# RWKV-7 recurrence in chunks of 64 tokens, with the triangular inverse from 16x16 blocks and two block doublings on TensorE

## The chip, the cores and the metric

The kernel runs on one core of a Trainium2 chip. The metric is the device time of one launch in microseconds. The engines are TensorE (PE in the rows, its weight loads PEld), VectorE (DVE), ScalarE (ACT), GpSimd (POOL) and SyncE (SP), which here only issues transfers.

## The reference, cut to what matters

A decoder layer on 1024 tokens: a projection, then a dilated attention branch and an RWKV-7 branch, which are gated, merged and projected. The change touches the RWKV branch alone, and in it the recurrence over the tokens, for 8 heads of 64 channels:

```
def rwkv7_scan(r, decay, k, v, a_in, b_in):
    def step(state, inp):
        r_t, w_t, k_t, v_t, a_t, b_t = inp
        sa = jnp.einsum('bhvk,bhk->bhv', state, a_t)
        state = (state * w_t[:, :, None, :] + sa[..., None] * b_t[:, :, None, :]
                 + v_t[..., None] * k_t[:, :, None, :])
        y = jnp.einsum('bhvk,bhk->bhv', state, r_t)
        return state, y
    _, ys = lax.scan(step, s0, xs)
```

with a_in = -kk and b_in = kk * a. The kernel does this in chunks of C tokens. Inside a chunk the tokens' influence on one another is a triangular system: with the strictly triangular C x C matrix of products of kk and kk * a (weighted with the decays), the contributions u of the chunk are the inverse of (one minus that matrix) times a right hand side made from the state and from v. So for each head and chunk a unit triangular matrix of C x C is inverted, ahead of the chain, since it depends on no state.

## The kernel before, in words

`start` normalises x and transposes it, `bias_table` builds tables, `rwkv` does the RWKV branch, `attention` and `finish` do the rest. In `rwkv` the 1024 tokens are 8 segments of SEG = 128, each of CPS = SEG / C = 4 chunks of C = 32. Heads are held in pairs (NPAIR = 4), one head on partitions 0 to 63, the other on 64 to 127.

For each segment s there are five steps. `rwkv_inputs` makes r, k, v, decays and the normalised kk: matmuls L495, L447, L451 and L456, with work of VectorE, ScalarE and GpSimd between them, in single buffers named kk, aa, c, q, sig and so on (`t_`). `rwkv_gram` makes ar and bk, multiplies them for each chunk and head (L557, 32 matmuls, in two halves), masks the products into gt (L558) and inverts. The inverse before: gt's triangular quarter goes to DRAM (L562, tin_d) and comes back with one matrix of 32 x 32 on each of 32 partitions (L565, xinv); 30 pairs of VectorE instructions, L570 (multiply into xtmp) and L572 (add into xinv), eliminate column by column; the result goes to DRAM (L575, x_d) and comes back as tt, laid out for TensorE (L578). `rwkv_rows` transposes bw and v (L593, L600) into bkt and uv (L597, L603), and has the bonus (L605). `rwkv_chain` goes through the chunks in order: right hand side from uv and the state (L626, L629), copied to rhs_s (L632, L633); u = tt times it (L636), copied to uv (L638, L639); the new state (L642, L645); y (L647, L650). Each of these is 8 matmuls, one for each head, which the trace shows as 16 records (a float32 matmul has two; a transpose has one). `rwkv_post` normalises y and stores it (L662 to L678).

The order is made by a scheduler, from priorities: in round i the chain of segment i has the highest, then come post of i - 1, rows of i + 1, inputs and gram of i + 2. What TensorE does beside it is projection work for later stages, called fill here: matmuls of 128 x 512 (L146), 624 of which are tied to the chain by `issue_after`, spread evenly over the marks that `rwkv_chain` returns (four for each chunk), 78 for each segment. A projection over half of the tokens, in records of 256 columns (L161), and the first fills run ahead of the chain. Each engine takes its instructions in the order that the scheduler wrote. PSUM has three buffers for the matmuls of inputs, gram, rows and post (ps_g), and one for y (ps_y).

Of the kernel before, what the change touches and what calls it, by code (L numbers as in the profile page):

```python
# [17 lines left out]
P = 128  # L18
# [4 lines left out]
NH = 8  # L23
# [11 lines left out]
C = 32  # L35
# [39 lines left out]
def constant_tables():  # L75
# [13 lines left out]
    i = np.arange(P)[:, None] % 64  # L89
    t = np.arange(64)[None, :]  # L90
    src, dst = i % 32, t % 32
    gmask = (np.where(t < 32, src < dst, src <= dst) * np.where(i < 32, -1.0, 1.0)).astype(np.float32)
# [4 lines left out]
    return dict(onehot=onehot.reshape(32, 1152), fill=fill.reshape(1, 1152), gmask=gmask, sel=sel.reshape(8, 512))  # L97


class Kernel:  # L100
# [154 lines left out]
    def small_loads(self):  # L255
# [28 lines left out]
        self.gmask = self.small.tile([P, 64], F32, name="gmask")  # L284
        nc.sync.dma_start(self.gmask, a["gmask"])
# [27 lines left out]
    def rwkv(self):  # L313
# [5 lines left out]
        with ExitStack() as ctx:  # L319
# [8 lines left out]
            nc.vector.memset(self.sgn, 1.0)  # L328
            nc.vector.memset(self.sgn[0:32], -1.0)
            nc.vector.memset(self.sgn[64:96], -1.0)  # L330
# [23 lines left out]
            for i in range(3):  # L354
                self.gt.append(rc.tile([P, NPAIR, CPS, 2, C], F32, name=f"gt{i}"))
            for i in range(2):
                self.tt.append(rc.tile([P, NPAIR, CPS, C], F32, name=f"tt{i}"))
            self.st = self.rw.tile([P, NPAIR, HD], F32, name="state", tag="state", bufs=2)
# [3 lines left out]
            raw = self.rw.tile([P, 1 + S], F32, name="waraw", tag="xinv")  # L362
# [158 lines left out]
    def rwkv_gram(self, sg):  # L521
# [26 lines left out]
        halves = (slice(0, 64), slice(64, 128))  # L548
        nh = NH * CPS
        tin_d = self.dram.tile([nh, C, C], F32, name=f"tin_d{s}")  # L550
        gm = self.gmask.rearrange("p (b t) -> p b t", t=C)[:, None].to_broadcast([P, 2 * CPS, 2, C])
        for p0 in (0, 2):
            ps = self.ps_g.tile([P, 2, CPS, 2 * C], F32, name="pg", tag="pg")
            for p in range(2):
                for ch in range(CPS):
                    for h in halves:
                        nc.tensor.matmul(ps[h, p, ch], bk[h, p0 + p, ch], ar[h, p0 + p, ch], start=True, stop=True)  # L557
            nc.vector.tensor_tensor(gt[:, p0:p0 + 2].rearrange("p a c b t -> p (a c) b t"),  # L558
                                    ps.rearrange("p a c (b t) -> p (a c) b t", t=C), gm, ALU.mult)
        for h in range(2):  # L560
            i0 = h * nh // 2
            nc.sync.dma_start(tin_d[i0:i0 + nh // 2].rearrange("c s t -> s c t"),  # L562
                              gt[h * 64:h * 64 + C, :, :, 0].rearrange("p a c t -> p (a c) t"))
        x = self.rw.tile([nh, C, C], F32, name="xinv", tag="xinv", bufs=1)
        nc.sync.dma_start(x, tin_d)  # L565
        tm = self.rw.tile([nh, 240], F32, name="xtmp", tag="xtmp", bufs=1)
        for j in range(1, C - 1):
            n = C - 1 - j
            o = tm[:, :j * n].rearrange("p (m n) -> p m n", n=n)
            nc.vector.tensor_tensor(o, x[:, 0:j, j:j + 1].to_broadcast([nh, j, n]),  # L570
                                    x[:, j:j + 1, j + 1:].to_broadcast([nh, j, n]), ALU.mult)
            nc.vector.tensor_tensor(x[:, 0:j, j + 1:], x[:, 0:j, j + 1:], o, ALU.add)  # L572
        nc.vector.memset(x.rearrange("p s t -> p (s t)")[:, 0:C * C:C + 1], 1.0)
        x_d = self.dram.tile([nh, C, C], F32, name=f"x_d{s}")
        nc.sync.dma_start(x_d, x)  # L575
        for h in range(2):
            i0 = h * nh // 2
            nc.sync.dma_start(tt[h * 64:h * 64 + C].rearrange("p a c t -> p (a c) t"),  # L578
                              x_d[i0:i0 + nh // 2].rearrange("c s t -> s c t"))
        sg.update(ar=ar, gt=gt, bw=bw, tt=tt)  # L580

    def rwkv_rows(self, sg):
# [4 lines left out]
        bkt = self.rw.tile([P, NPAIR, CPS, HD], F32, name="bkt", tag="bkt", bufs=2)  # L587
        uv = self.rw.tile([P, NPAIR, CPS, HD], F32, name="uv", tag="uv", bufs=2)
        for p0 in (0, 2):
            ps = self.ps_g.tile([P, 2, CPS // 2, 2, HD], F32, name="pg", tag="pg")  # L590
            for p in range(2):
                for j in range(CPS // 2):
                    nc.tensor.transpose(ps[:, p, j].rearrange("p h c -> p (h c)"),  # L593
                                        bw[p0 // 2][:, p, 2 * j:2 * j + 2].rearrange("p c t -> p (c t)"), self.ident)
            for par, rows in enumerate(halves):
                for h, out in enumerate(halves):
                    nc.scalar.activation(bkt[out, p0:p0 + 2, par::2], ps[rows, :, :, h], AF.Copy, scale=self.sgn[rows])  # L597
# [3 lines left out]
        for ch in range(CPS):  # L601
            for h in range(2):
                nc.scalar.copy(uv[64 * h + C:64 * h + 2 * C, :, ch], ps[ch * C:ch * C + C, :, h * HD:h * HD + HD])  # L603
# [464 lines left out]
```

## Time and profile before

| what | us |
|---|---|
| median of 3 runs | 1517.81 (1513.37 to 1521.56) |
| profiled execution | 1511.61 |
| its span | 1509.8 |

The page's mean granted clock of TensorE is 0.959 of full speed. Over the whole span TensorE is busy for 1391.1 us (92%), VectorE for 927.6 (61%), ScalarE for 583.7 (39%), GpSimd for 526.8 (35%). Busy shares over the whole span mix stages; the recurrence is the stretch from about 123 to 618 us, and what is done to it is read there. "Idle before" in a row is the time in which the engine stood still just ahead of it, with the instruction or transfer that ended it. The clock of a window is the mean granted one: 1.00 is 2.4 GHz, 0.50 is 1.2 GHz.

### The profile page before, as it was taken

The numbers are of one execution on the slowest core, as the hardware profiler recorded it, in microseconds if no ns is written. First come the engines' busy times: TensorE is split into PE (matmuls) and PEld (weight loads), VectorE is DVE, ScalarE is ACT, GpSimd is POOL, SyncE is SP. The second block draws the span as 40 slices with busy tenths as digits, with TensorE's granted clock in tenths as the row PEclk, the third lists the DMA queues.
The fourth block names the chain that finished last, engine by engine and source line by source line (L and its number), as shares of the span: only waits on it lengthen the run. The fifth ranks groups of instructions, "written<-read, shape, count | busy, mean of one in ns | idle before, by whom it ended". The sixth has DMA issues, their size and how long they took to land.

```text
span 1509.8 us, 24964 instructions
## 1 busy us (share of the span) xinstructions
PE 1391.1 (92%) x9566; PEld 1148.4 (76%) x9566; DVE 927.6 (61%) x1930; ACT 583.7 (39%) x1361; POOL 526.8 (35%) x418
## 2 busy tenths in 40 slices
PE   4989988999879989999999899989998999898997
PEld 3889876777657667787887788768876888786886
DVE  5213888869787784355548754875477447846723
ACT  4435472555526543134432543354235422002311
POOL 1347644355346343232222322222123123553300
PEclk9999998998879899999999999999999999999999
DMA  7665333121122122221112111221122114674306
GB/s 161 162 189 148 107 99 99 57 72 46 54 64 62 48 54 58 87 56 43 35 45 69 54 49 40 59 69 43 37 63 67 29 43 157 202 236 147 98 26 170
DMA packets 180715, 128.36 MB, mean 85 GB/s; under 512 B 35428, under 2 KB 160828, under 8 KB 180596
## 3 DMA queue, kind: packets, MB, share of 16 engines
q1 hardware_dynamic: 180596, 126.77, 30.4%
q8 instruction: 75, 1.23, 0.4%
q14 instruction: 44, 0.36, 0.1%
HBM read 99.13 MB, written 32.32 MB: 87 GB/s over the span
## 4 chain that ended last, share of the span: by engine, by line
PE 58%; DVE 20%; DMA 10%; ACT 4%; issue 3%; POOL 2%; SPq 1%; DVEq 0%; POOLq 0%; ACTq 0%
PE acc L146 32%; PE acc L161 4%; DMA wb<-wd 3%; DVE xtmp L570 3%; DVE xinv L572 2%; PE acc L1009 2%; PE acc L1010 2%; PE acc L1008 2%; DMA wstage<-in_w_in_dram 2%; DVE q L759 1%; PE rhs L647 1%; PE pw L855 1%; DMA wstage<-in_w_out_dram 1%; PE upd L636 1%; DVE L L782 1%
## 5 line engine op out<-in xcount | busy, mean ns | idle before, releaser
L125 POOL TENSOR_TENSOR wlo<-wstage,whi 128x512 fp32r<-128x512 f32 x186 | 255.0, 1373 | 545.2 <-DVE whi L122 294.7
L146 PE MATMUL acc<-hh,whi 128*128 128x512 f32 x976 | 398.2, 408 | 12.4 <-DVE q L759 7.5
L146 PE MATMUL acc<-hh,wlo 128*128 128x512 f32 x976 | 395.8, 406 | 0.9 <-POOL wlo L125 0.9
L146 PE MATMUL acc<-hl,whi 128*128 128x512 f32 x976 | 394.6, 405 | 0.0
L146 PEld LDWEIGHTS acc<-hh,whi 128*128 128x128 f32 x976 | 188.6, 193 | 52.9 <-issue 6.6
L146 PEld LDWEIGHTS acc<-hh,wlo 128*128 128x128 f32 x976 | 188.4, 193 | 39.4 <-POOL wlo L125 1.8
L146 PEld LDWEIGHTS acc<-hl,whi 128*128 128x128 f32 x976 | 188.5, 193 | 37.6 <-issue 0.3
L570 DVE TENSOR_TENSOR xtmp<-xinv 32x30 f32<-32x30 f32 (+14 forms) x240 | 115.6, 482 | 24.1 <-DMA xinv<-tin_d 18.3
L788 ACT ACTIVATE L<-L,nm 128x128 f32<-128x128 f32 (+1 forms) x192 | 83.8, 438 | 80.4 <-DVE nm L785 80.1
L782 DVE CUSTOM_DVE_ANT_0 L<-pw,bias 128x128 f32<-128x128 f32 (+1 forms) x192 | 62.3, 348 | 83.3 <-PE pw L781 82.8
L572 DVE TENSOR_TENSOR xinv<-xinv,xtmp 32x30 f32<-32x30 f32 (+14 forms) x240 | 109.8, 457 | 6.0
L122 DVE CAST whi<-wstage 128x512 fp32r<-128x512 f32 x108 | 54.5, 505 | 63.1 <-PE acc L146 26.4
L161 PE MATMUL acc<-hh,wlo 128*128 128x256 f32 x384 | 81.3, 294 | 5.4 <-POOL wlo L125 5.4
L767 POOL CAST k<-k 64x512 fp32r<-64x512 f32 x48 | 47.2, 982 | 106.3 <-ACT k L766 105.4
L124 ACT CAST whi<-wstage 128x512 fp32r<-128x512 f32 x78 | 48.2, 619 | 91.0 <-PE acc L161 30.7
L161 PE MATMUL acc<-hl,whi 128*128 128x256 f32 x384 | 83.1, 295 | 0.0
L161 PE MATMUL acc<-hh,whi 128*128 128x256 f32 x384 | 81.1, 293 | 0.2 <-ACT whi L124 0.2
L758 ACT ACTIVATE q<-acc 64x512 fp32r<-64x512 f32 x48 | 41.9, 907 | 94.1 <-PE pw L781 67.0
L858 ACT CAST ph<-pw 128x512 fp32r<-128x512 f32 x72 | 41.5, 578 | 84.5 <-PE pv L867 64.1
L780 PE MATMUL pw<-k,q 128*128 128x128 f32 (+1 forms) x192 | 52.1, 286 | 20.3 <-DVE st L782 20.1
L161 PEld LDWEIGHTS acc<-hh,wlo 128*128 128x128 f32 x384 | 61.9, 197 | 7.1 <-POOL wlo L125 6.0
L859 DVE TENSOR_TENSOR pl<-pw,ph 128x512 fp32r<-128x512 f32 x72 | 47.9, 670 | 30.9 <-ACT ph L858 30.5
(220 smaller groups left out, 2604.8 us busy)
## 6 DMA issues: line engine op xcount, KB each, us to landing
wstage<-in_w_in_dram SPq DMA_DIRECT2D x170, 256.0 KB
x<-in_x_dram SPq DMA_DIRECT2D x32, 256.0 KB
raw<-raw_d SPq DMA_DIRECT2D x24, 258.0 KB
raw_d<-rv SPq DMA_DIRECT2D x24, 256.0 KB
wb<-wd SPq DMA_DIRECT2D x24, 256.0 KB
bias_d<-bias_r SPq DMA_DIRECT2D x24, 192.0 KB
tb_d<-tb SPq DMA_DIRECT2D x16, 256.0 KB
ga_d<-tb SPq DMA_DIRECT2D x16, 256.0 KB
```

Of the source, the lines that this page charges most:

```text
L122: self.nc.vector.tensor_copy(hi, x)
L124: self.nc.scalar.copy(hi, x)
L125: self.nc.gpsimd.tensor_tensor(lo, x, hi.bitcast(F32), ALU.subtract)
L146: nc.tensor.matmul(ps, wt, x[:, k], start=k == 0 and j == 0, stop=k == KT - 1 and j == 2)
L161: nc.tensor.matmul(ps[:, half * 256:half * 256 + 256], wt, part(half, x, k), start=k == 0 and j == 0 and half == 0, stop=k == KT - 1 and j ...
L570: nc.vector.tensor_tensor(o, x[:, 0:j, j:j + 1].to_broadcast([nh, j, n]), x[:, j:j + 1, j + 1:].to_broadcast([nh, j, n]), ALU.mult)
L572: nc.vector.tensor_tensor(x[:, 0:j, j + 1:], x[:, 0:j, j + 1:], o, ALU.add)
L767: nc.gpsimd.tensor_copy(self.gview(ks2[h][b], g, half), hi.bitcast(F32))
L780: nc.tensor.matmul(ps[:, :w], qs2[h][:, qc], ks2[h][:, kc], start=True, stop=False)
L782: nc.vector.tensor_tensor_reduce(l[:, l0:l0 + w], ps[:, :w], self.bias[h][:, bo:bo + w], 1.0, -3.0e38, ALU.add, ALU.max, st[:, gi, 0, h, n ...
L788: nc.scalar.activation(ls, ls, AF.Exp, bias=nm[:, n:n + 1], scale=1.0, accum_out=st[:, gi, 1, h, n:n + 1])
L859: nc.vector.tensor_tensor(pl[:, :cw], ps[:, :cw], ph[:, :cw].bitcast(F32), ALU.subtract)
```

## The change

C becomes 64, so CPS becomes 2. A chunk's matrices are 64 x 64; the masks and the layouts of gt, uv, bkt follow, and the two heads of a pair lie crosswise, so that one matmul of the chain takes 64 rows and 128 columns (L677) and the state's part comes in two halves (L681). The marks for the fill are four for each chunk as before, so eight for each segment instead of sixteen. PSUM: ps_g has two buffers, y has two (rhs0, rhs1).

The inverse is a function of its own. The 64 x 64 matrices (16 in a segment) are cut into their four 16 x 16 diagonal blocks, which go to 64 partitions (four loads, L592) and are eliminated in 14 pairs of VectorE instructions (L597, L599). The blocks go back to DRAM (four stores, L602) into an x_d that is zero elsewhere, and come in as xd in TensorE's layout (L606). Then two doublings: transpose on VectorE (L608), multiply with gt (L612), mask (L613), multiply (L616), add (L617): now there are blocks of 32; transpose (L619), multiply (L623), copy (L626), multiply (L629), copy (L632): blocks of 64. These tiles take buffers that exist already: xd that of kk, xt that of aa, xq that of c, xinv that of ys. The diff's core:

```diff
-C = 32
+C = 64
-            self.ps_g = pool(name="ps_g", bufs=3, space=PSUM)
+            self.ps_g = pool(name="ps_g", bufs=2, space=PSUM)
-                self.gt.append(rc.tile([P, NPAIR, CPS, 2, C], F32, name=f"gt{i}"))
+                self.gt.append(rc.tile([P, 2, NPAIR, CPS, 2 * C], F32, name=f"gt{i}"))
+            self.x_d = [self.dram.tile([NH * CPS, C, C], F32, name=f"x_d{i}") for i in range(2)]
...
-            ps = self.ps_g.tile([P, 2, CPS, 2 * C], F32, name="pg", tag="pg")
-            for p in range(2):
-                for ch in range(CPS):
-                    for h in halves:
-                        nc.tensor.matmul(ps[h, p, ch], bk[h, p0 + p, ch], ar[h, p0 + p, ch], start=True, stop=True)
+            ps = [self.ps_g.tile([P, 2, CPS, 2 * C], F32, name="pg", tag="pg") for _ in range(2)]
+            for p, ch, i, j in itertools.product(range(2), range(CPS), range(2), range(2)):
+                for h in range(2):
+                    u, w = (own[i], own[1 - i])[h], (own[j], own[1 - j])[h]
+                    nc.tensor.matmul(ps[h][u, p, ch, w], bk[own[h], p0 + p, ch, own[1 - i]],
+                                     ar[own[h], p0 + p, ch, own[1 - j]], start=True, stop=True)
...
-        x = self.rw.tile([nh, C, C], F32, name="xinv", tag="xinv", bufs=1)
-        nc.sync.dma_start(x, tin_d)
+        x = self.rw.tile([nb * nm, 16, 16], F32, name="xinv", tag="ys")
+        block = lambda d, j: d[:, 16 * j:16 * j + 16, 16 * j:16 * j + 16]
+        for j in range(nb):
+            nc.sync.dma_start(x[j * nm:(j + 1) * nm], block(tin_d, j))
-        for j in range(1, C - 1):
-            n = C - 1 - j
+        for j in range(1, 15):
+            n = 15 - j
             o = tm[:, :j * n].rearrange("p (m n) -> p m n", n=n)
...
-        nc.sync.dma_start(x_d, x)
+        for j in range(nb):
+            nc.sync.dma_start(block(x_d, j), x[j * nm:(j + 1) * nm])
+        sq = lambda name, tag: self.rw.tile([P, NPAIR, CPS, C], F32, name=name, tag=tag)
+        d, dt, qt = sq("xd", "kk"), sq("xt", "aa"), sq("xq", "c")
         for h in range(2):
-            i0 = h * nh // 2
-            nc.sync.dma_start(tt[h * 64:h * 64 + C].rearrange("p a c t -> p (a c) t"),
-                              x_d[i0:i0 + nh // 2].rearrange("c s t -> s c t"))
+            nc.sync.dma_start(rows(d, h), half(x_d, h))
+        nc.vector.transpose(flat(dt), flat(d))
+        ps = psum()
+        for p, ch, h in each:
+            nc.tensor.matmul(ps[own[h], p, ch], gt[own[h], h, p, ch, own[h]], dt[own[h], p, ch], start=True, stop=True)
+        nc.vector.tensor_tensor(qt, ps, self.lmask[:, None, None].to_broadcast([P, NPAIR, CPS, C]), ALU.mult)
+        ps = psum()
+        for p, ch, h in each:
+            nc.tensor.matmul(ps[own[h], p, ch], qt[own[h], p, ch], d[own[h], p, ch], start=True, stop=True)
+        nc.vector.tensor_tensor(tt, ps, d, ALU.add)
+        dt = sq("xt", "aa")
+        nc.vector.transpose(flat(dt), flat(tt))
+        ps, qt = psum(), sq("xq", "c")
+        for p, ch, h in each:
+            nc.tensor.matmul(ps[hi[h], p, ch, 0:32], gt[lo[h], h, p, ch, hi[h]], dt[lo[h], p, ch, 0:32], start=True,
+                             stop=True)
+        for h in range(2):
+            nc.scalar.copy(qt[hi[h], :, :, 0:32], ps[hi[h], :, :, 0:32])
+        ps = psum()
+        for p, ch, h in each:
+            nc.tensor.matmul(ps[lo[h], p, ch, 32:64], qt[hi[h], p, ch, 0:32], tt[hi[h], p, ch, 32:64], start=True,
+                             stop=True)
+        for h in range(2):
+            nc.scalar.copy(tt[lo[h], :, :, 32:64], ps[lo[h], :, :, 32:64])
...
+            for p, h, w, u in each:
+                nc.tensor.matmul(py[h][:, p], gt[u, h, p, ch, w], uv[w, p, h, ch], start=p == 0, stop=False,
+                                 skip_group_check=True)
```

The change moves instructions on every engine. On TensorE, in the middle of the recurrence (segment 3 to 7 alike), before: the transposes of post and rows (L672, L593) stand between pieces of a chain (L642, L647) and fill (L146).

```order
L146 MATMUL acc<-hh_123,wlo 128x512
L647 MATMUL rhs<-uv,gt_428 32x64
L642 MATMUL snew<-uv,bkt 64x64 x8
L647 MATMUL rhs<-uv,gt_428 32x64 x6
L672 MATMUL pg<-ident,d 128x128 x4
L593 MATMUL pg<-ident,bw 128x128 x8
L647 MATMUL rhs<-uv,gt_428 32x64
L146 MATMUL acc<-hh_123,whi 128x512
```

The same place now: the last fill (L154), the four steps of an inverse (L612 to L629), rows (L644 to L655) and the first two steps of the chain that uses this inverse (its gt is the same, gt_429).

```order
L154 MATMUL acc<-hl_126,whi 128x512
L612 MATMUL pg<-xt,gt_429 64x64 x16
L616 MATMUL pg<-xd,xq 64x64 x16
L623 MATMUL pg<-xt,gt_429 32x32 x16
L629 MATMUL pg<-tt_431,xq 32x32
L725 MATMUL pg<-ident,d 128x128 x4
L629 MATMUL pg<-tt_431,xq 32x32 x15
L644 MATMUL pg<-ident,bw 128x128 x8
L650 MATMUL pg<-ident,v 128x128 x4
L655 MATMUL pg<-r,blk 128x512
L677 MATMUL rhs<-uv,gt_429 128x64 x4
L681 MATMUL rhs<-state,ar 64x64 x7
```

No matmul of the chain or of the fill stands between the steps of the inverse any more. On SP's queue, before: an inverse's two stores and one load go out, other transfers follow (tables L423, post L678, weights L113), then the store and the two loads of its result.

```order
L562 DMA tin_d_4660<-gt_428 32x16x32 x2
L565 DMA xinv<-tin_d_4660 32x1024
L423 DMA tb_d<-tb 128x512
L678 DMA orw_d<-ys 128x4x128
L113 DMA wstage<-in_w_in_dram 128x4x128
L423 DMA tb_d<-tb 128x512
L113 DMA wstage<-in_w_in_dram 128x4x128
L575 DMA x_d_4763<-xinv 32x1024
L578 DMA tt_430<-x_d_4763 32x16x32 x2
```

SP's queue now, at the same place in a segment.

```order
L121 DMA wstage<-in_w_in_dram 128x4x128
L588 DMA tin_d_5397<-gt_427 64x8x64 x2
L437 DMA tb_d<-tb 128x512
L592 DMA xinv<-tin_d_5397 16x16x16 x4
L602 DMA x_d_432<-xinv 16x16x16 x4
L606 DMA xd<-x_d_432 64x8x64 x2
L731 DMA orw_d<-ys 128x4x128
```

The store of x_d follows the load of xinv directly, post's store (L731) comes behind the loads of xd, and an inverse has twelve transfers in place of six.

## Rows read from the trace of the kernel before

**Rows 1.** Windows: length, busy of each engine (instructions), PEclk, DMA share, GB/s.

```profile
206.00:618.00 412.00, 373.86 (x3999) 286.11 (x3997) 305.41 (x701) 195.86 (x475) 182.35 (x155) 0.91 0.23 63
```

**Rows 2.** Timeline of TensorE, the ends of stages: start, length, instruction, records.

```profile
123.43 1.71 PE L495 MATMUL pg<-wa,waup 64*128 64x128 f32 x16
...
149.87 2.08 PE L557 MATMUL pg<-ar,bk 64*64 64x64 f32 x64
...
206.50 0.68 PE L629 MATMUL rhs<-state,ar 64*64 64x64 f32 x16
...
278.40 0.68 PE L626 MATMUL rhs<-uv,gt 32*64 32x64 f32 x16
...
618.03 0.63 PE L647 MATMUL rhs<-uv,gt 32*32 32x64 f32 x14
```

**Rows 3.** Groups, 206 to 618 us, VectorE: busy, mean ns, idle before.

```profile
L570 DVE TENSOR_TENSOR xtmp<-xinv 32x30 f32<-32x30 f32 (+14 forms) x210 | 97.7, 465 | 20.8 <-DMA xinv<-tin_d 16.0
L572 DVE TENSOR_TENSOR xinv<-xinv,xtmp 32x30 f32<-32x30 f32 (+14 forms) x210 | 93.6, 446 | 5.2
```

**Rows 4.** Waits of TensorE, 206 to 575 us: total, times, longest.

```profile
PE upd L636 <- DVE rhs_s L632: 16.5, 8, 4.1
```

**Rows 5.** Chain of work that ended last: start, length, what.

```profile
380.64 2.73 DMA x_d<-xinv
...
383.85 2.15 DMA tt<-x_d
...
435.54 2.57 DMA tin_d<-gt
438.17 2.20 DMA xinv<-tin_d
...
441.12 0.22 DVE xinv L572
441.37 0.24 DVE xtmp L570
```

**Rows 6.** Groups with shapes kept apart, 206 to 618 us.

```profile
L558 DVE TENSOR_TENSOR gt<-pg,gmask 128x512 f32<-128x512 f32 x12 | 8.0, 679 | 0.8 <-PE pg L557 0.8
L503 DVE TENSOR_TENSOR_SCAN c<-smask,sig 128x512 f32<-128x512 f32 x6 | 7.2, 1208 | 0.0
L603 ACT COPY uv<-pg 32x256 f32<-32x256 f32 x56 | 20.4, 364 | 0.7
```

**Rows 7.** Timeline of TensorE, inside segments.

```profile
397.80 2.15 PE L495 MATMUL pg<-wa,waup 64*128 64x128 f32 x16
...
427.56 2.08 PE L557 MATMUL pg<-ar,bk 64*64 64x64 f32 x64
...
499.77 0.93 PE L593 MATMUL pg<-ident,bw 128*128 128x128 f32 x7
...
505.16 1.16 PE L495 MATMUL pg<-wa,waup 64*128 64x128 f32 x8 [0.45 <-ACT bkt L597]
...
616.18 0.39 PE L146 MATMUL acc<-hl,whi 128*128 128x512 f32 x1
616.41 0.40 PE L146 MATMUL acc<-hh,wlo 128*128 128x512 f32 x1
```

**Rows 8.** Timeline of SP's queue.

```profile
495.13 0.86 SPq L562 DMA_DIRECT2D tin_d<-gt  x2
497.93 0.31 SPq L565 DMA_DIRECT2D xinv<-tin_d  x1
```

**Rows 9.** Windows around a wait of TensorE, columns as in rows 1.

```profile
379.00:386.00 7.00, 0.39 (x2) 0.17 (x2) 2.80 (x9) 0.99 (x2) 2.68 (x2) 0.75 0.54 131
386.00:394.00 8.00, 7.87 (x64) 6.47 (x65) 5.52 (x17) 5.03 (x12) 2.79 (x3) 0.58 0.23 68
```

**Rows 10.** Timeline of TensorE at that wait.

```profile
385.47 0.39 PE L636 MATMUL upd<-rhs_s,tt 32*32 32x64 f32 x2 [6.98 <-DMA tt<-x_d]
386.13 1.03 PE L636 MATMUL upd<-rhs_s,tt 32*32 32x64 f32 x14 [0.28 <-DMA tt<-x_d]
```

More of the change, by code (lines that the diff above doesn't have):

```diff
@@ L582, in rwkv_rows @@
+        for h in range(2):
+            nc.scalar.copy(tt[lo[h], :, :, 32:64], ps[lo[h], :, :, 32:64])
     def rwkv_rows(self, sg):
@@ L586, in rwkv_rows @@
         halves = (slice(0, 64), slice(64, 128))
[L587 to L597, printed above, removed]
+        bkt = self.rw.tile([P, NPAIR, 2, CPS, HD], F32, name="bkt", tag="bkt", bufs=2)
+        uv = self.rw.tile([P, NPAIR, 2, CPS, HD], F32, name="uv", tag="uv", bufs=2)
+        for ch in range(CPS):
+            ps = self.ps_g.tile([P, NPAIR, P], F32, name="pg", tag="pg")
+            for p in range(NPAIR):
+                nc.tensor.transpose(ps[:, p], bw[p // 2][:, p % 2, ch], self.ident)
+            nc.scalar.activation(bkt[:, :, 1, ch], ps[:, :, HD:], AF.Copy, scale=self.sgn)
+            nc.scalar.activation(bkt[halves[1], :, 0, ch], ps[halves[0], :, 0:HD], AF.Copy, scale=-1.0)
+            nc.scalar.copy(bkt[halves[0], :, 0, ch], ps[halves[1], :, 0:HD])
         ps = self.ps_g.tile([P, NPAIR, SEG], F32, name="pg", tag="pg")
@@ L602, in rwkv_rows @@
             for h in range(2):
[L603 removed]
+                nc.scalar.copy(uv[halves[h], :, h, ch], ps[halves[ch], :, h * HD:h * HD + HD])
         ps = self.ps_g.tile([P, NPAIR, SEG], F32, name="pg", tag="pg")
@@ L614, in rwkv_chain @@
         sg["yt"] = yt
-        hs = ((slice(0, 64), slice(0, 32), slice(32, 64)), (slice(64, 128), slice(64, 96), slice(96, 128)))
-        each = [(p, *h) for p in range(NPAIR) for h in hs]
+        own = (slice(0, C), slice(C, 2 * C))
+        each = [(p, h, own[h], own[1 - h]) for p in range(NPAIR) for h in range(2)]
         marks = []
@@ L628, in rwkv_chain @@
-            for p, h, u, w in each:
-                last = nc.tensor.matmul(py[h, p], ar[h, p, ch], st[h, p], start=False, stop=False,
-                                        skip_group_check=True)
-            marks.append(last.ins)
-            nc.vector.tensor_copy(rs[0:C], py[0:C])
-            nc.scalar.copy(rs[64:64 + C], py[64:64 + C])
+            for p, h, w, u in each:
+                nc.tensor.matmul(py[h][:, p], gt[w, h, p, ch], uv[w, p, h, ch], start=p == 0, stop=False,
+                                 skip_group_check=True)
@@ L634, in rwkv_chain @@
+            for part in range(2):
+                for p, h, w, u in each:
+                    last = nc.tensor.matmul(py[h][(u, w)[part], p], ar[w, p, ch, own[part]], st[w, p], start=False,
+                                            stop=False, skip_group_check=True)
+                if part == 0:
+                    marks.append(last.ins)
+            nc.vector.tensor_copy(rs[own[0]], py[1][own[0]])
+            nc.scalar.copy(rs[own[1]], py[0][own[1]])
             ps = self.ps_ch.tile([P, NPAIR, HD], F32, name="upd", tag="ch")
-            for p, h, u, w in each:
+            for p, h, w, u in each:
@@ L645, in rwkv_chain @@
             nc.vector.tensor_tensor(sn, ps, sw, ALU.add)
-            for p, h, u, w in each:
-                last = nc.tensor.matmul(py[w, p], gt[u, p, ch, 1], uv[u, p, ch], start=False, stop=True,
+            for p, h, w, u in each:
+                last = nc.tensor.matmul(py[h][w, p], gt[u, h, p, ch, w], uv[u, p, h, ch], start=False, stop=True,
                                         skip_group_check=True)
-            for i, (_, _, w) in enumerate(hs):
-                nc.scalar.copy(yt[ch * C:ch * C + C, :, i], py[w])
+            for h in range(2):
+                nc.scalar.copy(yt[ch * C:ch * C + C, :, h], py[h][own[h]])
             self.st = sn
```

83 lines of the change are left out of this document (49 added, 34 removed).

## The prediction

> **What bounds the kernel now.** I read the windows first, to find the stage, then the timeline of TensorE, to see what paces it, then the groups and waits, to see who is late. The recurrence and its inverses run from the first matmul of `rwkv_inputs` at 123.4 us to the last y matmul (L647) at 618.0 [rows 1, 2]. What follows on TensorE follows at once and is not touched by the change, so a shift of that end moves the total by as much. The chain starts at 206.5 and closes eight segments in 412 us, 51.5 us a segment [rows 1, 2]. In these 412 us TensorE is busy for 374, VectorE for 305, at a mean granted clock of 0.91 [rows 1]. Of VectorE's 305 us the inverse alone (L570 and L572, 7 segments) has 97.7 + 93.6 = 191 us, some 27 us a segment [rows 3]. The chain waits for VectorE in consequence: `upd` waited 16.5 us in all for the rhs_s copy [rows 4]. So neither engine is the bound alone. TensorE's work fills most of it, and the waits of the chain fill the rest. What keeps it at 51.5 is that three segments are in flight: the inverse of s+2 runs beside the chain of s.
>
> **The change part by part.**
>
> *VectorE.* 60 small steps a segment become 28. Two steps follow each other in 0.25 us [rows 5], so 28 take about 6.5 us where about 27 went: some 20 us a segment are taken off VectorE. It gains two more gt evacuations, a multiply, an add (0.68 each, L558's row) and two transposes [rows 6]. No transpose is in the trace. Between a 32x256 copy of 0.36 us and a 128x512 scan of 1.21 us [rows 6] I take 0.9, since its operands are 128x512.
>
> *The chain.* Per 64 tokens 2 x 5 bursts of 16 records become 6 bursts, of which L677 has tiles of 64 by 128. A full burst takes 0.61 us from the start of one to the next (L626 at 278.40, 0.68 us long) [rows 2]; L677 lies between that and the 1.71 us of L495, whose tiles are 64 by 128 with 128 columns for 64 [rows 2]. I take 0.86, near half of L495, and 4.3 us for a chunk of 64 tokens. As to small tiles, 16 records at 32x64 (278.40) and 16 at 64x64 (206.50) both took 0.68 [rows 2], so going from tiles of 32 to tiles of 64 costs nothing by the rows. The Trainium skill, in TensorEngine Tiling (Array Packing), section Key Properties, has different tiles loading weights and multiplying in parallel, and section Overview counts 16 tiles at 32x32 and 4 at 64x64. By that rule alone L677, with two tiles for four, would take 1.2 us instead of my 0.86, some 6 us over 16 chunks, and the trace, where 8 and 4 tiles took the same time, does not bear it out.
>
> *The gram.* Twice the matmuls: 128 records a segment for 64, which took 2.08 [rows 7]: 4.2 us, and the gt evacuation of the later half, 2 x 0.68 = 1.4, before the inverse may load.
>
> *The order.* This is the heart of it. The tiles of the new inverse, xd, xt, xq and xinv, lie in the buffers kk, aa, c and ys, which `rwkv_inputs` and `rwkv_post` write. So the inputs of segment s+1 can't write aa, kk and c before the inverse of s is done with them, and the order after shows what that brings: in each of segments 3 to 7 the inverse of s stands last, right behind the second half of its gram and 17 or 19 fill matmuls; then come rows of s and the chain of s, with the inputs and the gram of s+1 among them. Before, the inverse of s+2 ran while the chain of s had TensorE. Now nothing of TensorE lies beside the round trip through DRAM but 4 us of fill (19 x 0.23, the fill's distance from 616.18 to 616.41 [rows 7]). One period is a loop through five things, and I sum them from the end of one inverse to the end of the next.
>
> H, from the end of the inverse to the first input matmul: before, L593 at 499.77 to L495 at 505.16, 5.4 us, for the same transposes and evacuations [rows 7].
>
> I, from that matmul to the end of the second gram half. At the stage's beginning, with no chain beside it, 123.43 to 149.87, 26.4 us, to the start of the gram [rows 2]; in a busy segment 397.80 to 427.56, 29.8 [rows 7]; plus the gram's 4.2 with half its work on the first half. TensorE's own list in it comes to the same: 61 fill x 0.23 = 14, two chunks of the chain without the fill 8.6, the inputs' matmuls 4, the gram 4.2. I take 32, between 27 and 36.
>
> G, the gt evacuation: 1.4.
>
> R, the round trip. Before: 435.54 (tin_d) to the first step behind the load, 4.8 us (2.57 + 2.20 and their joints); back, 380.64 to 386.0, 5.4 us [rows 5]. An issue on SP takes 0.31 to 0.43 [rows 8]; three more loads of xinv and three more stores of x_d stand in a row, 2 x 3 x 0.43 = 2.6. With 28 steps, 6.5: 19.3. The pieces are 64 bytes now in place of 128 for tin_d and 4 KB for xinv. In the trace the 128-byte pieces landed in 2.57 us and the 4-KB rows in 2.20 [rows 5], 0.4 apart, so I add nothing. The Trainium skill, in DMA: Bandwidth & Descriptors, section Specifications, says that transfers under 512 B are read, modified and written. By that rule the four passes would be dearer, by 0.4 each if the trace's difference is its price, 1.6 us a segment; no row shows more.
>
> T, the first transpose: 0.9.
>
> S, four bursts of 32 records (L612, L616, L623, L629) with a multiply, an add, a transpose and 2 x 2 copies of 0.36 [rows 6] between them, each step waiting for the one ahead. At the full clock a burst takes 1.24 (twice 0.61). But TensorE has then waited some 18 us. Before, it waited 6.98 us for the same transfer to tt, and the granted clock of the next 8 us was 0.58, mostly the lower level of 1.2 GHz; 14 records went in 0.96 us, 0.069 each [rows 9, 10]. So 32 records take 2.2 us: 8.8 + 0.68 + 0.68 + 0.9 + 1.4 + 1.0 for seven joints of 0.15 = 13.5 (9.6 at the full clock).
>
> P = 5.4 + 32 + 1.4 + 19.3 + 0.9 + 13.5 = 72.5 us a segment, for 51.5 now. The 20 us that VectorE is relieved of don't appear: its steps were beside the chain, and what they cost there, 16.5 us of waiting in all, is less than one period's growth.
>
> *The first segments.* Gram 0 starts at 149.9 as now, with 25 fill records of the span's 256 columns (0.115 each, half of 0.23) between its halves, and ends at 157; gt 158.4; R + T to 178.6; TensorE comes to L612 by 157 + 202 x 0.115 = 180; S with 84 such records among it: the inverse of segment 0 ends at 198. Segment 1: inputs to gram 26.4, gram and gt 5.6, R + T + S 33.7: 262 to 264. Segment 2 is the first full period, and has 19 fills before its end: 337. So the inverse of 7 ends at 337 + 5 x 72.5 = 699.5. Behind it 4 us of rows and two chunks of 39 fills (9.0) and 4.3 each: 730 us. Before it was 618. That is +112.
>
> **Sum.** 1511.6 us, the profiled run, + 112 = 1623. The median shown is 0.4% above that run; 6 us are inside the range.
>
> **The rivals.** *Slower, but less: the clock stays at 2.4 GHz.* Then S is 9.6 and I 28: P 64.6, the end near 682, 1576 us. For it: the clock recovered within 8 us before [rows 9]. Against: every period has its own wait of 18 us.
>
> *Slower, and more: each pass in small pieces is dearer*, by 1 us for each of the six added DMAs: P 78.5, 1653 us. For it: nothing in the trace has 64-byte pieces.
>
> *Faster: the round trip is covered.* If the inverse of s lies beside the chain of s-1 as now, the loop is set by TensorE's list: about 32 for I, 5.4 for the rows, 7.5 for the bursts of the inverse and what of G is left: P 45. End: 337 + 225 + 30.6 = 593, 26 us earlier, 1486. It decides at P = (618 - 30.6 - 337) / 5 = 50.1: G + R + T + S would have to fall from 35 to 13. For it: VectorE is relieved of 20 us and `upd` waited 16.5 for it [rows 3, 4]. Against: the shared buffers forbid it, and the order has no chain matmul beside the round trip.
>
> *No change*: P between 48.6 and 51.6 by both at once, part covered and part not. Nothing speaks for just this.
>
> **How the numbers follow.** Forecast (P 66 to 76, some 1590 to 1641) 0.72; the full clock 0.11; dearer pieces 0.10; faster 0.04; no change 0.03. For the range I take the bounds: P = 61 (I 27, R 17 with the issues hidden, S 9.6) gives 1566, P = 84 (I 36, R 24, S 15.5, H 6.5) gives 1681. Half a per cent, 7.6 us, is about what a measurement of this kernel can tell from no change. Faster by more 0.04, within 0.03, slower 0.93.
>
> **What would show it.** In the trace of the changed kernel: segments of the chain 65 to 80 us apart; TensorE idle for 15 to 20 us ahead of each L612, ended by the transposed xd or its DMA; a clock near 0.5 in the bursts behind it; VectorE's L597 and L599 at some 45 us for seven segments, in unbroken rows of 0.25 us; burst L677 near 0.86. Wrong it would be if chain matmuls fill the time ahead of L612, if the load behind tin_d lands in much over 3 us, or if inputs to gram take under 25 us once VectorE is free.

## The result and the profile after

The changed kernel takes 1693.3 us (median of 4 runs, 1684.77 to 1697.18), the kernel before 1519.7 beside it: a ratio of 1.114, interval 1.108 to 1.120. The forecast was 1623, range 1566 to 1681. The direction was right and the loss much larger, +174 us for a forecast +112.

The loss lies in the recurrence alone. Its last y matmul ends at 803 us where [rows 2] had 618, and the stretch behind it is as long as before. Windows of the changed kernel (length, busy of PE, PEld, DVE, ACT, POOL with instructions, clock, DMA share, GB/s), the stage from the old start of the chain to its end, and the rest:

```profile
206.00:803.00 597.00, 440.19 (x4366) 351.12 (x4364) 199.86 (x487) 170.08 (x423) 174.21 (x144) 0.72 0.17 43
803.00:1692.00 889.00, 844.69 (x4205) 702.78 (x4203) 523.39 (x1045) 294.26 (x716) 248.62 (x184) 0.98 0.28 81
```

Against [rows 1] TensorE is busy for 74% of the stage instead of 91%, at a clock of 0.72 instead of 0.91. VectorE is indeed relieved: 200 us in 597, for 305 in 412. What ends TensorE's idle time is one thing. Waits of TensorE from 120 to 800 us (total, times, longest), the first three:

```profile
PE pg L612 <- DVE xt L608: 120.3, 8, 21.7
PE pg L623 <- DVE xt L619: 11.4, 7, 1.6
PE pg L568 <- POOL bk L550: 7.3, 1, 7.3
```

And the timeline of L612, segments 3, 4, 5 and 7 (start, length, instruction, records, idle before):

```profile
430.31 1.97 PE L612 MATMUL pg<-xt,gt 64*64 64x64 f32 x32 [18.02 <-DVE xt L608]
510.17 1.97 PE L612 MATMUL pg<-xt,gt 64*64 64x64 f32 x32 [18.47 <-DVE xt L608]
593.68 1.97 PE L612 MATMUL pg<-xt,gt 64*64 64x64 f32 x32 [20.35 <-DVE xt L608]
...
753.53 1.76 PE L612 MATMUL pg<-xt,gt 64*64 64x64 f32 x28 [15.97 <-DVE xt L608]
```

Four segments from 430.31 to 753.53: 80.8 us each, and 16 to 22 us of each are an idle TensorE, where the forecast expected it. One segment in the prediction's parts, as windows: H, the two pieces of I (split where the clock changes), R with T, and S.

```profile
442.60:450.30 7.70, 7.42 (x32) 4.91 (x32) 0.81 (x2) 3.84 (x10) 2.71 (x3) 0.50 0.11 34
450.30:466.00 15.70, 15.70 (x88) 13.32 (x87) 3.10 (x7) 7.05 (x19) 5.39 (x4) 0.59 0.11 34
466.00:488.30 22.30, 22.30 (x311) 17.89 (x309) 13.64 (x22) 6.29 (x14) 14.36 (x13) 1.00 0.23 63
...
490.00:510.20 20.20, 1.73 (x10) 1.12 (x9) 6.14 (x31) 0.00 (x0) 0.00 (x0) 0.60 0.22 45
510.20:522.40 12.20, 8.48 (x136) 7.02 (x136) 3.48 (x5) 5.36 (x14) 1.19 (x1) 0.50 0.00 1
```

R and S are as forecast. H and I are not: after the idle TensorE the clock stays at its lower level of 1.2 GHz through S, through H and through the first half of I, some 30 us, until well after TensorE is busy without a gap (15.70 us of 15.70, at 0.59). The round trip itself, in the chain of work that ended last (start, length, what):

```profile
490.15 2.62 DMA tin_d<-gt
...
494.20 2.01 DMA xinv<-tin_d
...
497.56 0.21 DVE xtmp L597
497.79 0.21 DVE xinv L599
...
503.96 1.70 DMA x_d<-xinv
...
506.38 2.83 DMA xd<-x_d
...
509.31 0.72 DVE xt L608
```

### The profile page after: what moved, and what is told of

Read it like the earlier page. It is cut to its first block, busy times and chain, and to the rows that moved or that the text cites. A ratio compares the mean times of both kernels' runs of the same rounds, so it can differ in the third digit from the quotient of the medians.

```text
span 1692.7 us, 25693 instructions
## 1 busy us (share of the span) xinstructions
PE 1463.2 (86%) x10078; PEld 1220.8 (72%) x10078; DVE 789.9 (47%) x1674; ACT 549.6 (32%) x1281; POOL 508.3 (30%) x402
## 4 chain that ended last, share of the span: by engine, by line
PE 52%; DVE 16%; DMA 9%; ACT 4%; issue 2%; SPq 2%; POOL 1%; DVEq 0%; ACTq 0%; POOLq 0%
PE acc L154 29%; DMA wb<-wd 2%; PE rhs L677 2%; PE acc L1062 2%; PE acc L1063 2%; PE acc L1061 2%; PE rhs L681 2%; DMA tin_d<-gt 1%; DMA wstage<-in_w_out_dram 1%; DVE q L812 1%; PE pw L908 1%; DVE xinv L599 1%; DMA xd<-x_d 1%; DVE xtmp L597 1%; PE pg L509 1%
## 5 line engine op out<-in xcount | busy, mean ns | idle before, releaser
L154 PE MATMUL acc<-hh,whi 128*128 128x512 f32 x976 | 403.2, 413 | 12.1 <-DVE q L812 7.1
L154 PE MATMUL acc<-hh,wlo 128*128 128x512 f32 x976 | 399.4, 410 | 0.4 <-POOL wlo L133 0.3
L154 PE MATMUL acc<-hl,whi 128*128 128x512 f32 x976 | 397.2, 407 | 0.0
L154 PEld LDWEIGHTS acc<-hh,whi 128*128 128x128 f32 x976 | 191.5, 196 | 53.1 <-PE pw L908 5.2
L154 PEld LDWEIGHTS acc<-hh,wlo 128*128 128x128 f32 x976 | 191.6, 196 | 40.3 <-POOL wlo L133 1.6
L154 PEld LDWEIGHTS acc<-hl,whi 128*128 128x128 f32 x976 | 191.5, 196 | 37.8 <-issue 0.9
L612 PE MATMUL pg<-xt,gt 64*64 64x64 f32 x256 | 15.2, 305 | 120.3 <-DVE xt L608 120.3
L612 PEld LDWEIGHTS pg<-xt,gt 64*64 64x64 f32 x256 | 13.9, 212 | 122.8 <-issue 114.3
L169 PE MATMUL acc<-hl,whi 128*128 128x256 f32 x384 | 79.6, 287 | 0.0
L729 POOL TENSOR_TENSOR ys<-ys,bv 128x512 f32<-128x512 f32 x8 | 10.2, 1272 | 173.9 <-ACT ys L728 173.9
```

The lines of the kernel that those rows point to most:

```text
L154: nc.tensor.matmul(ps, wt, x[:, k], start=k == 0 and j == 0, stop=k == KT - 1 and j == 2)
L169: nc.tensor.matmul(ps[:, half * 256:half * 256 + 256], wt, part(half, x, k), start=k == 0 and j == 0 and half == 0, stop=k == KT - 1 and j ...
```

## The experiments

**What closes the loop: SBUF or PSUM.** The prediction said that the inverse shares SBUF buffers with the inputs. There is a second tie: the new inverse has four PSUM tiles, and takes them from the two pg buffers that gram, rows, post and inputs use. They are handed out in the order in which the code is written: inverse of s+1, then rows of s+1, then inputs of s+2. So the inputs can't have a tile until the inverse is done with its last. Three kernels tell the two apart. All have two accumulators of the fill for three, which pays for the PSUM bank where one is taken. Here and below, a time without a range was measured once.

```diff
# e1_own_sbuf
-            for i in range(3):
+            for i in range(2):
...
-        x = self.rw.tile([nb * nm, 16, 16], F32, name="xinv", tag="ys")
+        x = self.rw.tile([nb * nm, 16, 16], F32, name="xinv", tag="xinv")
-        d, dt, qt = sq("xd", "kk"), sq("xt", "aa"), sq("xq", "c")
+        d, dt, qt = sq("xd", "xd"), sq("xt", "xt"), sq("xq", "xq")
# e2_own_psum
+            self.ps_i = pool(name="ps_i", bufs=1, space=PSUM)
-        psum = lambda: self.ps_g.tile([P, NPAIR, CPS, C], F32, name="pg", tag="pg")
+        psum = lambda: self.ps_i.tile([P, NPAIR, CPS, C], F32, name="pi", tag="pi")
# e3_own_both: both edits
```

> The changed kernel with buffers of their own in SBUF for xd, xt, xq and xinv (room for them: two gt buffers for three); and two accumulators of the fill for three, so that it stands beside the next two runs. Theory A, that of the prediction: the loop is closed by the shared SBUF buffers (kk, aa, c, ys). Then the inputs of s+1 run beside the inverse of s, a segment takes 50 to 60 us for the 81 of the changed kernel, and the total is 1540 to 1590. Theory B: the loop is closed by PSUM. The inverse takes its four PSUM tiles from the two pg buffers that gram, rows, inputs and post use too, and they are handed out in program order, so the inputs of s+1 wait for the last tile of the inverse of s whatever SBUF does. Then nothing changes: 1675 to 1710, segments of 80 to 83 us.

> The changed kernel with a PSUM bank of its own for the four tiles of the inverse (taken from the fill's accumulators, two for three); SBUF buffers shared as they are. Theory A: nothing changes, 1675 to 1710. Theory B: rows and the first input matmuls of s+1 (L509) no longer wait for the inverse of s, but aa, c and kk are still shared, so the rest of the inputs does: segments of 58 to 68 us, 1570 to 1630.

> Both: SBUF buffers of their own for the inverse and a PSUM bank of its own. Theory A: as the run with SBUF buffers alone, 1540 to 1590. Theory B: only this one opens the loop altogether: the inverse of s+1 lies beside the chain of s, TensorE has work through the round trip and keeps the full clock, segments of 45 to 53 us, 1490 to 1540. If 81 us a segment came from the dearer work itself and not from the loop, it stays above 1620.

Measured: 1692.7, 1562.3 and 1484.7 us. Own SBUF buffers alone change nothing, and L612 waits nearly as before (109.7 us from 200 to 800 us, for 116.2 in the same window of the changed kernel). An own PSUM bank alone takes 131 us off, though the SBUF buffers are still shared; theory B had expected a little less, 1570 to 1630. Both together open the loop, 1484.7 (1480.35 to 1486.76), a ratio to the kernel before of 0.975, interval 0.972 to 0.979: faster than both kernels, and just below the 1490 to 1540 expected. The waits of TensorE on L612 (200 to 800 us) in the first and in the third of them, and the windows of the third, stage and rest:

```profile
PE pg L612 <- DVE xt L608: 109.7, 6, 21.4
```

```profile
PE pi L612 <- DVE xt L608: 1.1, 2, 0.8
```

```profile
206.00:586.00 380.00, 352.91 (x4275) 290.60 (x4274) 196.64 (x476) 166.12 (x408) 165.23 (x139) 0.93 0.27 70
586.00:1483.00 897.00, 848.16 (x4212) 702.47 (x4210) 515.38 (x1044) 292.98 (x716) 240.81 (x184) 0.98 0.28 80
```

110 us of waiting become 1, the clock is 0.93, and the stage ends at 586, 33 us ahead of the kernel before. So theory B holds as to what closes the loop first; the shared SBUF buffers are a second lock, worth 78 us once the first is open (1562.3 to 1484.7).

**The same tie put into the old kernel.** If the order of the pg buffers is enough in itself, one tile of them behind the old inverse must do harm in the old kernel.

```diff
+        ps = self.ps_g.tile([P, NPAIR, CPS, C], F32, name="pg", tag="pg")
+        nc.tensor.matmul(flat(ps[0:C]), self.ident[0:C, 0:C], flat(tt[0:C]), start=True, stop=True)
         sg.update(ar=ar, gt=gt, bw=bw, tt=tt)
```

> The kernel before, with one thing more: behind each inverse a matmul reads tt and writes a tile of the pg buffers that nobody reads. The work added is 0.5 us a segment. Theory B (buffers handed out in program order): from then on the inputs of s+2 wait for the inverse of s+1 in the old kernel too, and its inverse is longer (round trip 10 us and 60 steps at 0.25 to 0.46): segments of 70 to 85 us for 51.5, total 1620 to 1760. Rival: three pg buffers absorb one tile, and it was the four steps of the new inverse that cost: 1505 to 1535.

Measured: 1689.3 us, +170, with 1 to 2 us of work added for a segment. The waits of TensorE (200 to 800 us) and two of the added matmuls in its timeline:

```profile
PE pg L582 <- DMA tt<-x_d: 120.4, 8, 30.6
```

```profile
520.04 1.91 PE L582 MATMUL pg<-tt,ident 32*32 32x512 f32 x2 [12.66 <-DMA tt<-x_d]
...
596.75 1.91 PE L582 MATMUL pg<-tt,ident 32*32 32x512 f32 x2 [19.27 <-DMA tt<-x_d]
```

A result that nobody reads makes the old kernel as slow as the changed one, by the same 120 us of waiting. This run doesn't separate two things: the added matmul holds a pg tile, and it also stands in TensorE's own queue, where whatever is behind it waits with it. The same matmul into a bank of its own wasn't run. That the handing out of pg is enough to close the loop rests on the run with a PSUM bank of its own and on the next one.

**The order, without a further bank.** If it is the order of handing out, then writing the doublings elsewhere must help with no further bank.

```diff
-        self.rwkv_inverse(s, gt, tt)
+        sg["inv"] = self.rwkv_inverse(s, gt, tt)
+        next(sg["inv"])
...
+        yield
         nc.vector.transpose(flat(dt), flat(d))
...
-ORDER = "prig"
+ORDER = "prixg"
+                        if what == "x" and i + 1 < NSEG:
+                            for _ in segs[i + 1]["inv"]:
+                                pass
```

> No PSUM bank of its own: the two pg buffers serve all as in the changed kernel, three accumulators of the fill as there. Only the program order differs: the doublings of s+1 (from the first transpose on) are written behind the inputs of s+2 and ahead of their gram, not ahead of both; SBUF buffers of its own (two gt buffers for three). Theory B: what closes the loop is the order in which the two buffers are handed out, so this opens it: segments of 45 to 55 us, 1480 to 1540. Rival: two buffers are too few for the inverse and the rest in any order: 1560 to 1690.

Measured: 1514.7 us (1510.81 to 1521.0), ratio to the kernel before 0.996, interval 0.993 to 0.999. The new order takes 179 us off the changed kernel, with its two pg buffers and three accumulators. Its SBUF buffers are its own. Alone they were worth nothing, but 78 us once PSUM was open, so the 179 belong to the order and to them together. It is 30 us slower than the kernel with a bank of its own. Why is not shown; gram, rows and the doublings still share the two buffers, and its longest wait of TensorE (200 to 700 us) is inside the doublings:

```profile
PE pg L636 <- ACT xq L633: 16.6, 4, 7.4
```

**The clock.** H and I were dearer than forecast, with a clock of 0.5 to 0.6 in them. Two kernels keep TensorE busy in the round trip by matmuls whose results are overwritten.

```diff
# e4_warm; e10_warm_all has 1, 2 and 1 more ahead of L616, L623 and L629
         ps = psum()
+        for _ in range(20):
+            nc.tensor.matmul(flat(ps), self.blk, gt[:, 1, 2:4].rearrange("q p c t -> q (p c t)"), start=True, stop=True)
```

> The changed kernel with 20 more matmuls of 128x128x512 on TensorE during each round trip, whose results are not used (they go to the PSUM tile that L612 overwrites). They take some 17 us and fit into the 20 us in which TensorE stands idle, so the loop is as it was; what differs is that TensorE isn't idle ahead of L612. If the granted clock after the wait is what makes H, I and S dearer: S falls from 12.2 to about 9, H from 8.2 to 5.5, I from 39 to about 33, segments of 68 to 72 us, total 1620 to 1645. If those parts are paced by the other engines: segments of 79 to 83 us, 1680 to 1710.

> As the run with 20 unused matmuls in the round trip, with four more between the steps of the inverse (one ahead of L616, two ahead of L623, one ahead of L629, sized by the waits of 0.5 to 1.6 us there). In the run with 20 the clock held through the round trip and fell again in those waits, and H stayed at 7.8. Theory: the lower clock from the inverse to the middle of I is what H and I were mis-sized by: H 5.4 to 6.5, I 32 to 35, segments of 70 to 73 us, 1635 to 1655. Rival: the clock is worth the 4 us a segment that the run with 20 gave and no more: 1670 to 1690.

Measured: 1680.1 and 1690.1 us. By the total both are misses: the clock of the stretch from 340 to 800 us rose from 0.70 (changed kernel) to 0.88 and 0.89, and next to nothing came of it. That stretch in the changed kernel and in the second run:

```profile
340.00:800.00 460.00, 339.77 (x3293) 269.62 (x3294) 148.95 (x353) 129.54 (x324) 127.17 (x107) 0.70 0.16 41
```

```profile
340.00:800.00 460.00, 433.15 (x3740) 304.67 (x3739) 151.83 (x361) 133.07 (x334) 129.92 (x109) 0.89 0.16 42
```

The windows say where it rose: in the round trip, where the added matmuls run and which is no shorter for it, and in S, which falls from 12.2 to 10.3 us in most segments. In H and the first half of I it hardly rose in three of the five segments from 3 to 7. H and the first half of I of segment 4 in the second run:

```profile
440.20:448.40 8.20, 7.36 (x33) 4.80 (x32) 1.55 (x3) 4.34 (x12) 3.29 (x3) 0.51 0.11 32
448.40:467.00 18.60, 18.60 (x106) 15.38 (x106) 3.10 (x7) 7.33 (x20) 5.39 (x4) 0.66 0.09 29
```

The changed kernel had 0.50 and 0.59 there. So in these segments the runs left the clock low just where it was to be tested. In segment 6 of the second run it did hold, and segment 5, with nearly the same work, differs by it. Windows, H and I of segment 5, H and I of segment 6:

```profile
519.30:527.50 8.20, 7.50 (x34) 4.91 (x32) 1.55 (x3) 4.33 (x12) 3.27 (x3) 0.50 0.11 32
527.50:569.40 41.90, 41.90 (x405) 34.55 (x405) 16.70 (x31) 13.94 (x34) 19.82 (x17) 0.78 0.21 54
603.60:609.40 5.80, 4.17 (x32) 2.81 (x32) 1.55 (x3) 4.29 (x11) 3.23 (x3) 1.00 0.16 45
609.40:644.20 34.80, 34.28 (x395) 27.82 (x393) 16.97 (x30) 12.15 (x31) 18.55 (x16) 0.90 0.13 39
```

439 records took 50.1 us at 0.50 and 0.78, and 427 took 40.6 at 1.00 and 0.90: H and I are worth some 9 us less at the full clock, and 40.6 is near the 37.4 of the forecast. So a lower clock does make them dearer, by this one pair of segments in a run that was timed once. What makes the clock fall again behind S isn't settled by these runs.

**The fill.** In the closed loop 61 fill matmuls stand in I, on the path, and TensorE is idle in R. The fill was tied to the last gram matmul of the next segment, which `rwkv_gram` keeps for it.

```diff
-                    self.mark = steps[u * len(steps) // n]
+                    self.mark = segs[i + 1]["last"] if i + 1 < NSEG else steps[u * len(steps) // n]
```

> The changed kernel, with the 78 fill matmuls of a segment tied to the last gram matmul of the next segment, in place of the marks of the chain: all of them then stand between the gram and the first step of the inverse, in the 20 us in which TensorE is idle. Theory: in the closed loop the fill is on the path in I (61 fills, 14 us at the full clock and more at half) and costs nothing in the round trip (78 x 0.23 = 18 us): I falls from 39 to 24 to 28, segments of 65 to 70 us, total 1600 to 1640. Rival: without fill the chain and the inputs wait for their own steps as long as the fill took, and the clock falls: I stays over 35, 1670 to 1710.

Measured: 1660.5 us, 33 less than the changed kernel, between the theories. H and I of segment 5, and its G and R:

```profile
510.90:516.90 6.00, 5.71 (x33) 3.65 (x33) 0.86 (x2) 3.85 (x11) 2.77 (x3) 0.69 0.15 44
516.90:548.60 31.70, 24.21 (x302) 22.10 (x303) 14.36 (x27) 8.86 (x25) 15.28 (x13) 0.63 0.13 27
548.60:571.20 22.60, 20.73 (x111) 16.90 (x110) 9.61 (x35) 5.41 (x10) 5.80 (x5) 0.92 0.40 105
```

I fell from about 39 to 31.7, not to 26: without fill TensorE is idle for 7.5 us of it (31.7 less 24.21 busy), and the clock in I is 0.63 where it was 0.59 and 1.00. It waits for the evacuation of the gram (L571) and for the chain's own copies (L687). L613 is here the first step of the inverse, ahead of which 30.4 us of idle time are left for 116.2 (waits of TensorE, 200 to 800 us):

```profile
PE pg L613 <- DVE xt L609: 30.4, 7, 7.6
PE pg L568 <- DVE gt L571: 19.7, 7, 4.9
...
PE upd L690 <- ACT rhs_s L687: 7.6, 5, 3.0
```

R has its work now. So moving the work helps, but the term I became about 7 us shorter and not 13: there are waits now that the fill used to cover, and the clock is low.

**L677.** Its burst was forecast at 0.86 us for a chunk. In the timeline of the changed kernel, the 16 records of one chunk in one run at the full clock, 8 of another's in a run at the lower clock, and 8 of a third's in a run at the full one:

```profile
292.36 1.11 PE L677 MATMUL rhs<-uv,gt 64*128 64x64 f32 x16
...
447.11 1.97 PE L677 MATMUL rhs<-uv,gt 64*128 64x64 f32 x8
...
471.38 1.10 PE L677 MATMUL rhs<-uv,gt 64*128 64x64 f32 x8
```

In 14 of the 16 chunks the burst stands in two halves of 8 records, with other matmuls between them: that makes 2.1 us a chunk at the full clock and 3.8 at the lower. The two chunks that have it in one run pay for 16 records what a run of 8 pays. In program order the matmuls of the two heads, on partitions 0 to 63 and 64 to 127, alternate; a run of 8 is presumably one head alone, which the rows don't name.

The next two runs cut the matmul in two. The edit:

```diff
-                nc.tensor.matmul(py[h][:, p], gt[w, h, p, ch], uv[w, p, h, ch], start=p == 0, stop=False,
+                for rows in own:
+                    nc.tensor.matmul(py[h][rows, p], gt[w, h, p, ch, rows], uv[w, p, h, ch], start=p == 0, stop=False,
```

> The changed kernel, with the first burst of a chunk (L677, 8 matmuls whose tiles are 64 by 128) written as 16 matmuls of 64 by 64, like L681 beside it. In the changed kernel a record of L677 takes 0.112 us at the full clock and 0.213 at half, so its 16 records 1.8 to 3.4 us a chunk, where the prediction had 0.86. Theory: the price comes from the tile of 64 by 128; then 32 records of 64 by 64 take 1.25 to 2.2, and 16 chunks save 9 to 19 us: 1672 to 1685. Rival: the price lies in the weights of 128 columns and stays when they are cut in two, or the chain waits there anyway: 1688 to 1700.

> SBUF and PSUM of its own for the inverse, and L677 in halves. If L677's price stands on TensorE's path in the open loop too, 16 chunks at the full clock save 0.55 each, 9 us: 1470 to 1480. If the open loop is paced by something else: 1480 to 1490, as with the two buffers alone.

Measured: 1690.5 us (ratio to the kernel before 1.111, interval 1.106 to 1.116, beside 1.108 to 1.120 of the changed kernel), and 1482.0 on the open version (0.9751, interval 0.972 to 0.978, beside 0.9752). The burst got cheaper as expected, the same half of it here, after the edit, at the lower clock:

```profile
447.03 1.12 PE L678 MATMUL rhs<-uv,gt 64*64 64x64 f32 x16
```

1.12 us for 1.97. But 3 us of 1690 and of 1482 are inside the intervals, so that it stood on the path is not shown. Nor is the price that of the 64 by 128 form as such, since uncut and in one run the burst costs half as much. In the open version at least 7 of the 16 chunks have it in one run already, as here at the full clock:

```profile
358.57 1.11 PE L677 MATMUL rhs<-uv,gt 64*128 64x64 f32 x16
```

**The inverse without the longer chunk.** The old chunks of 32 with the new kind of inverse: 16 by 16 blocks of the 32 matrices of a segment on 64 partitions, one doubling, own SBUF buffers and own PSUM bank.

```diff
+        for j in range(nb):
+            nc.sync.dma_start(x[j * nh:(j + 1) * nh], block(tin_d, j))
-        for j in range(1, C - 1):
+        for j in range(1, 15):
...
+            nc.tensor.matmul(ps[own[h], p, ch], gt[own[h], p, ch, 0], dt[own[h], p, ch], start=True, stop=True)
...
+            nc.tensor.matmul(ps[own[h], p, ch], qt[own[h], p, ch], d[own[h], p, ch], start=True, stop=True)
...
+            nc.vector.tensor_tensor(tt[own[h]], ps[own[h]], d[own[h]], ALU.add)
```

> The other half of the change alone: chunks of 32 as before, with the new kind of inverse (16x16 blocks on 64 partitions, one doubling on TensorE for 32x32), its own SBUF buffers and its own PSUM bank (two accumulators of the fill for three). Theory: what the open version gained over the kernel before (36 us) is VectorE's relief, 60 small steps to 28 and 16x16 operands: then this gives it too, 1475 to 1500. Rival: the gain is that of the longer chunk, half as many chunks in the chain: then this stays at 1508 to 1530.

> The kernel before with two accumulators of the fill for three, and nothing else: what the bank costs that the runs with a PSUM bank for the inverse took. If fill and the late stages need the third: 1525 to 1545, and then the chunks of 32 with the new inverse lost by the bank and not by the inverse. If not: 1510 to 1525, and their 1537 is the inverse's own matmuls and clock.

Measured: 1537.5 us (1534.7 to 1541.23), ratio 1.0125, interval 1.008 to 1.017: 1% slower than before, and above both ranges. The control with two accumulators gives 1522.6, ratio 1.0007, interval 0.998 to 1.003: in the old kernel the bank costs nothing. The stage from 206 to 635 us, first in the kernel before, then here:

```profile
206.00:635.00 429.00, 390.86 (x4087) 300.14 (x4086) 311.28 (x713) 198.73 (x482) 190.50 (x161) 0.92 0.24 64
```

```profile
206.00:635.00 429.00, 401.52 (x4904) 312.41 (x4902) 193.78 (x502) 192.70 (x469) 176.40 (x155) 0.88 0.23 59
```

VectorE loses 117 of 311 us and nothing is gained: TensorE has 800 records more in the same time at a lower clock, and its y matmuls end at 635 instead of 619. So VectorE's relief, at the price of the inverse's own matmuls, is worth nothing by itself here, and the 2.5% of the open version need the longer chunk, with half as many rounds of the chain.

## Why the prediction was right or wrong, point by point

**That the loop closes, and what it looks like: right.** From segment 3 on TensorE idles for 16 to 22 us ahead of each L612, ended by the transposed xd; VectorE's steps stand in unbroken rows, 0.23 us apart, and take 38 us for seven segments where 45 were expected; the segments are 81 us apart, 1 us above the expected 65 to 80.

**Why it closes: wrong.** The step "the tiles of the new inverse lie in the buffers kk, aa, c and ys" named a true tie that wasn't the one in force. The kernel had the other in it: `psum` takes from ps_g. The shared SBUF buffers alone, removed, gave 0 us, PSUM alone 131, the order (with SBUF) 179. With the tie that the prediction named left as the only one, the kernel takes 1562.3, 43 us over the kernel before and not 112, so that the forecast of a segment came as near as it did is partly luck. The rival "the round trip is covered" was rightly held unlikely, but its reason, that the shared buffers forbid it, was only the second of two. With both ties gone it came true, at 1484.7 against the 1486 worked out for it; its segments average (561.8 - 204.8) / 7 = 51 us and not 45, and its first segments are shorter than that rival took, so the agreement of the totals is partly luck.

**The terms of a segment.** G 1.4, forecast 1.4. R 19.6, forecast 19.3: with 64-byte pieces the load of xinv took 2.01 us and the store of x_d 1.70, no more than the 2.20 and 2.73 in [rows 5], where one transfer moved 128 KB and now each of four moves 16. By that the rule of the Trainium skill, in DMA: Bandwidth & Descriptors, section Specifications, on transfers under 512 B, shows no price here, and the rival of dearer pieces falls. Only these two passes have pieces of 64 bytes; the prediction misread tin_d and xd, whose pieces grew from 128 to 256 bytes. The transpose took 0.72, forecast 0.9; S 12.2, forecast 13.5.

**H and I: mis-sized.** H was 8.2 (mean of segments 3 to 7) for 5.4, I 39 for 32. These are the terms that made the segment 81.4 instead of 72.5. The rows that H came from and the 26.4 us of I were at the full clock, the 29.8 us of I at 0.83, and the window rows show the lower level through H and the first half of I. [rows 9] had shown the clock back within 8 us of a wait of 7 us; I took that recovery over for a wait of 18 us that is followed by a stretch of short bursts and waits, S, where it did not recover. The rival with the clock at the full level went the wrong way from there. Segment 6 of the run with 24 added matmuls, with H 5.8 and I 34.8 at 1.00 and 0.90, shows what is left without it: 3 us of the 10, of which L677 explains two chunks of 1.2.

**L677: mis-sized.** 0.86 us by half of L495; measured 2.1 at the full clock where the burst stands in two runs, 1.11 where it stands in one. In a run of 8 a record of 64 columns starts 0.112 us behind the last, about what L495's of 128 cost ([rows 2]: 1.71 for 16). The columns that stream through were not what set it, and the forecast took the burst as whole, which it was in 2 chunks of 16. The Trainium skill, in TensorEngine Tiling (Array Packing), section Tiling Modes, counts fewer tiles of this form than of 64 by 64. The 1.2 us that I worked out by it is near the 1.11 of a burst in one run, and short of the two runs.

**The first segments: a step left out.** I let segment 2 be "the first full period". It took 96 us, from 262.5 to 358.8, and the end of that inverse came 22 us later than forecast. TensorE's timeline between the end of the inverse of 1 and the first input matmul of 2:

```profile
261.66 2.01 PE L644 MATMUL pg<-ident,bw 128*128 128x128 f32 x8
264.11 1.12 PE L650 MATMUL pg<-ident,v 128*128 128x128 f32 x4 [0.44 <-ACT bkt L647]
265.37 2.08 PE L655 MATMUL pg<-r,blk 128*128 128x512 f32 x2
...
270.59 1.11 PE L644 MATMUL pg<-ident,bw 128*128 128x128 f32 x4
...
274.84 1.11 PE L644 MATMUL pg<-ident,bw 128*128 128x128 f32 x4
...
279.43 0.60 PE L650 MATMUL pg<-ident,v 128*128 128x128 f32 x4
280.19 0.68 PE L689 MATMUL upd<-rhs_s,tt 64*64 64x64 f32 x16
280.80 1.13 PE L655 MATMUL pg<-r,blk 128*128 128x512 f32 x2
```

The rows of segments 0 and 1 both stand there, with half a chunk of chain 0 and its fill: 21.6 us for an H of 5.4. By the code it is the same tie: the inverse of 1 is written ahead of the rows of 0, so these too take their pg tiles behind it.

**The sum.** Five segments by 8.9 us = 44.5, segment 2 by 22, the end behind the last inverse 37.4 us for 30.6, 7: 73 us, which is the 803 of the trace less the 730 of the forecast. Of these, the 81.4 us of a segment lie inside the range's own bounds, 61 to 84: put into the forecast's sum they give 337 + 407 + 30.6 = 775 us and a total of 1668, within 1566 to 1681. What took the time out of the range is the first period, for which it had no term of its own, with the longer end: 28 us. The first 14 us of that end were at a clock of 0.62, where the forecast had the full one.

## What to carry to other kernels

A step that is given tiles from a shared PSUM pool is tied to everything that takes from this pool after it in program order; look up who comes next in the ring before looking at times, since one unread tile, with the matmul that writes it, cost the old kernel 170 us here. To hide a round trip, give the step buffers of its own in SBUF and in PSUM alike, for either alone gave 0 and 131 of 209 us. And don't size what follows a long wait of TensorE at the full clock: here it was low through 12 us of bursts with waits between them and for some 20 us more.

## What the runs showed of the hardware

Eight float32 records on a tile of 64 by 128 in a run of their own took 1.10 us at the full clock and 1.97 at half, and sixteen in one run 1.11 at the full clock; cut into two of 64 by 64, the work of the eight took 1.12 us for 1.97 at half the clock. Pieces of 64 bytes, 16 KB a transfer, were no dearer than rows of 4 KB, 128 KB a transfer (2.01 and 1.70 us for 2.20 and 2.73). Matmuls that fill TensorE's idle time raised the mean granted clock from 0.70 to 0.89 in one stretch and shortened the kernel by no more than 3 us; behind them, in H of three segments of five, it was at 0.50 again.
